# Residual adds by column halves, the last norm in pieces, and reciprocal roots as a power on GpSimd, in a two-layer hybrid decoder trunk

## The chip, the core and the metric

The kernel runs on one core of a Trainium2 chip. The metric is the device time of one execution in microseconds, as the median of several runs. The engines are TensorE (PE in the profile; its weight loads are PEld), VectorE (DVE), ScalarE (ACT), GpSimd (POOL) and SyncE (SP), which here only issues DMAs. A q behind an engine's name (SPq, ACTq) is its sequencer, which issues DMAs and waits on semaphores.

## The reference

256 tokens of 1024 columns go through two layers. Layer 0 mixes with sparse attention in two head groups, layer 1 with multi-head latent attention; after each comes a channel mixer (PEER) that fetches from 16384 experts. Every part reads a root-mean-square norm of the residual x and adds its result to x; one more norm gives the output:

```python
def rms_norm(x, g):
    xf = x.astype(jnp.float32)
    y = xf * lax.rsqrt(jnp.mean(xf * xf, axis=-1, keepdims=True) + NORM_EPS)
    return (y * g.astype(jnp.float32)).astype(x.dtype)

    for i in range(DEPTH):
        h = rms_norm(x, attn_norm[i])
        x = x + mixer(h)          # even_mixer, then mla_mixer
        h = rms_norm(x, ffn_norm[i])
        x = x + peer_ffn(h, peer_w_q[i], peer_sub_keys[i], peer_u[i], peer_v[i])
    return rms_norm(x, final_norm)
```

The latent attention norms two inner vectors as well, one of 768 and one of 256 columns. So the kernel takes seven sets of reciprocal roots: four of x ahead of the four parts, two inner ones, and the last norm's.

## The kernel before

The residual stays in the core's memory as four tiles x[tb][j]: two blocks tb of 128 tokens, each in two column halves j of 512. All weights stream once from HBM (320 MB). `Weights` loads units of up to 1024 columns into three raw buffers and splits them half by half, four halves ahead, into two float32r parts hi (ScalarE, L69) and lo (VectorE, L70), five buffers of each kind. A product is three matmuls: hi times hi, hi times lo, lo times hi.

The four stages run one behind the other: `even_mixer`, `peer`, `mla_mixer`, `peer`. Each of them ends in the same way. The mixers (`OutProj`) and the channel mixer (`peer`, `mm`, L1069 to L1074) accumulate their output in four PSUM tiles, one for each (tb, j). The last two chunks, that is four halves of weights (chunk 1 j 0, chunk 1 j 1, chunk 2 j 0, chunk 2 j 1), go through `last4` (L82): all four for tb 0, and then all four for tb 1. After each token block `add_to_x` (L460) adds two accumulators to x on VectorE, one instruction for each j (L463). During tb 1 one more half is split after each product.

The next stage starts with `to_T` (L284): TensorE transposes chunks of 128 columns of x for both token blocks (L288), ScalarE and VectorE write them as hi and lo. The PSUM pool of a stage is closed before that of the next one is opened.

`x_rstd` (L270) takes the squares of x on ScalarE with sums (L275) and calls `rsqrt` (L248): on VectorE it scales the sums, makes a first guess by an integer shift, and takes three Newton steps, column by column. The result is used late: by the rope tables (`scaled`, L343) in the mixers, by the scores' copy (L1024) and the normed tokens (`normed`, L794 and L795) in `peer`. `mla_mixer` calls `rsqrt` for its inner norms (L672, L675).

At the end `finish` (L808) loads the last gain, calls `x_rstd` for each token block, multiplies x by the gain on GpSimd (L817, four products), scales one half on ScalarE (L820) and the other on VectorE (L821), and issues four stores on SP (L823).

The kernel is written with the Tile framework. It sets the semaphores and orders the instructions of each engine's queue by a planner: by readiness in a simulated time line and by priority, which is the order of the code, save that the splits are moved up by 100 (`HP`) and the adds onto x by 200. So an engine's order in the trace isn't always that of the code.

## Time and profile before

| | |
|---|---|
| median of 3 runs | 1945.64 us (1944.63 to 1948.22) |
| profiled execution, span | 1945.3 us |
| PE busy | 1917.9 us (99%) |
| DVE busy | 1454.4 us (75%) |
| ACT busy | 1264.2 us (65%) |
| POOL busy | 6.4 us, 10 instructions |
| HBM read | 319.97 MB, 165 GB/s over the span |

The span goes from the first to the last instruction of one execution. A busy engine is one that has an instruction in flight, so PE's 99% counts the time in which it is fed, and also that in which its clock is granted at half rate. What can be taken out of the span is above all the time in which PE has nothing. The stages lie in the span at about 0 to 148 us (mixer of layer 0), to 980 (PEER), to 1101 (mixer of layer 1), to 1934 (PEER), and the rest is the last norm.

### The profile page before, as it was taken

What the parts mean: (1) busy time and instruction counts of PE and PEld (TensorE: products, weight loads), DVE (VectorE), ACT (ScalarE), POOL (GpSimd) and SP (SyncE); (2) the same over time, 40 slices, a digit from 0 to 9 for tenths busy, and PEclk for the clock granted to TensorE, in tenths of its full rate; (3) what the DMA queues carried; (4) which work ended last, traced back from release to release, by engine and by line L of the source; (5) the groups of instructions that cost most, each with busy time, mean ns of one, the idle gap of its engine ahead of it and who ended that gap; (6) DMA issues with size and microseconds to landing.
All of it is one profiled execution on the core that took longest, in us unless ns stands there. A gap on an engine that the chain in (4) does not pass through costs nothing.

```text
span 1945.3 us, 35740 instructions
## 1 busy us (share of the span) xinstructions
PE 1917.9 (99%) x12588; PEld 1727.7 (89%) x12588; DVE 1454.4 (75%) x3710; ACT 1264.2 (65%) x3060; POOL 6.4 (0%) x10
## 2 busy tenths in 40 slices
PE   8999999999999999999999999999999999999997
PEld 7769999999999888888888799999999998888886
DVE  7958998777788666666687699977778876666665
ACT  5556567887777555555576664688877765555554
POOL 0000000000000000000000000000000000000001
PEclk9989999999999999999999999999999999999999
DMA  6425565444444555555554345654444456666664
GB/s 186 128 65 164 172 195 166 154 151 152 152 152 153 194 192 190 192 192 190 189 168 131 120 150 177 195 163 152 144 152 152 154 171 191 190 194 193 188 193 141
DMA packets 90179, 323.33 MB, mean 166 GB/s; under 512 B 10512, under 2 KB 10896, under 8 KB 89744
## 3 DMA queue, kind: packets, MB, share of 16 engines
q1 hardware_dynamic: 88704, 318.71, 51.4%
q8 instruction: 99, 1.62, 0.3%
q0 software_dynamic: 288, 2.10, 0.3%
q14 instruction: 80, 0.66, 0.1%
q10 hardware_dynamic: 1008, 0.25, 0.1%
HBM read 319.97 MB, written 1.05 MB: 165 GB/s over the span
## 4 chain that ended last, share of the span: by engine, by line
PE 94%; DVE 3%; DMA 1%; ACT 1%; issue 1%; ACTq 0%; DVEq 0%
PE S L804 13%; PE S L805 13%; PE S L806 13%; PE acc L1072 12%; PE acc L1073 12%; PE acc L1074 12%; PE scp L984 6%; PE pj L301 2%; PE pj L303 2%; PE pj L302 2%; PE bk L372 1%; DVE lo L70 1%; DMA raw<-in_pu 1%; PE pj L438 1%; PE scp L1021 1%; PE pj L439 1%
## 5 line engine op out<-in xcount | busy, mean ns | idle before, releaser
L69 ACT ACTIVATE hi<-raw 128x512 fp32r<-128x512 f32 (+2 forms) x1214 | 763.2, 634 | 589.8 <-DVE lo L70 196.5
L70 DVE TENSOR_TENSOR lo<-raw,hi 128x512 fp32r<-128x512 f32 (+2 forms) x1214 | 827.1, 686 | 377.4 <-ACT hi L69 368.5
L804 PE MATMUL S<-hi,hi 128*128 128x256 f32 x2048 | 584.2, 285 | 1.9 <-ACT A L1013 1.8
L806 PE MATMUL S<-hi,lo 128*128 128x256 f32 x2048 | 573.4, 280 | 0.5 <-DVE lo L70 0.3
L805 PE MATMUL S<-lo,hi 128*128 128x256 f32 x2048 | 572.9, 280 | 0.0
L804 PEld LDWEIGHTS S<-hi,hi 128*128 128x128 f32 x2048 | 389.4, 190 | 3.1 <-ACT A L1013 2.9
L806 PEld LDWEIGHTS S<-hi,lo 128*128 128x128 f32 x2048 | 386.4, 189 | 1.3 <-DVE lo L70 1.2
L805 PEld LDWEIGHTS S<-lo,hi 128*128 128x128 f32 x2048 | 387.3, 189 | 0.0
L1073 PE MATMUL acc<-lo,ohA 128*128 128x512 f32 x512 | 200.2, 391 | 0.0
L1073 PE MATMUL acc<-lo,ohB 128*128 128x512 f32 x512 | 200.2, 391 | 0.0
L1074 PE MATMUL acc<-hi,ohA 128*128 128x512 f32 x512 | 199.4, 390 | 0.0
L1074 PE MATMUL acc<-hi,ohB 128*128 128x512 f32 x512 | 198.7, 390 | 0.0
L1072 PE MATMUL acc<-hi,ohB 128*128 128x512 f32 x512 | 160.5, 393 | 0.0
L1072 PE MATMUL acc<-hi,ohA 128*128 128x512 f32 x512 | 160.5, 393 | 0.0
L984 PE MATMUL scp<-ohA,ohB 128*128 128x128 f16 x1024 | 143.1, 296 | 0.0
L951 ACT ACTIVATE ohB<-ohB,RA 128x128 bf16<-128x128 bf16 x256 | 134.5, 654 | 0.0
L1074 PEld LDWEIGHTS acc<-hi,ohB 128*128 128x128 f32 x512 | 96.1, 188 | 22.0
L1074 PEld LDWEIGHTS acc<-hi,ohA 128*128 128x128 f32 x512 | 96.1, 188 | 22.0
L1072 PEld LDWEIGHTS acc<-hi,ohA 128*128 128x128 f32 x512 | 96.2, 188 | 20.8
L1072 PEld LDWEIGHTS acc<-hi,ohB 128*128 128x128 f32 x512 | 96.2, 188 | 20.7
L1073 PEld LDWEIGHTS acc<-lo,ohA 128*128 128x128 f32 x512 | 96.2, 188 | 20.3
L1073 PEld LDWEIGHTS acc<-lo,ohB 128*128 128x128 f32 x512 | 96.2, 188 | 20.2
(263 smaller groups left out, 2524.8 us busy)
## 6 DMA issues: line engine op xcount, KB each, us to landing
raw<-in_pu SPq DMA_DIRECT2D x256, 512.0 KB, 3.6
raw<-in_pv SPq DMA_DIRECT2D x256, 512.0 KB, 4.1
raw<-in_pq SPq DMA_DIRECT2D x32, 512.0 KB, 3.5
raw<-in_w SPq DMA_DIRECT2D x20, 512.0 KB, 3.7
raw<-in_uq SPq DMA_DIRECT2D x9, 512.0 KB, 4.3
raw<-in_w SPq DMA_DIRECT2D x12, 352.0 KB, 2.9
raw<-in_w0o SPq DMA_DIRECT2D x8, 512.0 KB, 3.6
raw<-in_w1o SPq DMA_DIRECT2D x8, 512.0 KB, 3.5
```

What stands on the lines that cost most here:

```text
L69: self.nc.scalar.activation(hi[:, :w], src, AF.Copy)
L70: self.nc.vector.tensor_tensor(lo[:, :w], src, hi[:, :w].bitcast(F32), op=OP.subtract)
L301: nc.tensor.matmul(ps[tb], hi[c][:, t], a, start=st, stop=False)
L302: nc.tensor.matmul(ps[tb], hi[c][:, t], b, start=False, stop=False)
L804: nc.tensor.matmul(p, a, hi[c], start=first and i == 0, stop=False)
L805: nc.tensor.matmul(p, a, lo[c], start=False, stop=False)
L806: nc.tensor.matmul(p, b, hi[c], start=False, stop=last and i == 3)
L951: nc.scalar.activation(e[:, :, j], e[:, :, j], AF.Relu, bias=r[1], scale=r[2])
L984: nc.tensor.matmul(p[:, i], E[:, 1, :, i], G[:, s, :, i], start=i + s == 0, stop=True, skip_group_check=True)
L1072: nc.tensor.matmul(o, a[:, 0, t], w[0], start=b == 0, stop=False)
L1073: nc.tensor.matmul(o, a[:, 0, t], w[1], start=False, stop=False)
L1074: nc.tensor.matmul(o, a[:, 1, t], w[0], start=False, stop=b == NK - 1)
```

## The change

Four things are changed; docstrings and comments are left out too, which changes nothing.

`last4` goes by column halves: for j 0 the two halves of weights of that j for tb 0 and then for tb 1, then the same for j 1. After each pair (tb, j) one accumulator is added to x. The next weights are still split during tb 1, now two in the first column half and two in the second.

`rsqrt` runs on GpSimd: it adds the parts, scales them and adds the epsilon, and raises the result to the power -0.5. VectorE's Newton steps are gone.

`finish` gives back a function that is called after each add onto x: the square and the sum of that piece, for j 0 the product with the gain on GpSimd, and for j 1 the root, the scaling of both halves and the stores. The second half is multiplied by root and gain in one instruction of VectorE.

The stores go out on two queues, the first column half's on ScalarE's, the second's on SP's.

```diff
     def last4(self, products):
-        j = self.pos
+        k = self.pos
         w = [self.next(self.look - i) for i in range(4)]
-        for tb in range(2):
-            for i in range(4):
-                products(i, w[i], tb)
-                if tb == 1:
-                    self.split(j + self.look + 1 + i)
-            yield tb
+        for j in range(2):
+            for tb in range(2):
+                for i in (j, j + 2):
+                    products(i, w[i], tb)
+                    if tb == 1:
+                        k += 1
+                        self.split(k + self.look)
+                yield tb, j
...
+        mhalf = cp.tile([128, 1], F32, name="mhalf")
+        nc.gpsimd.memset(mhalf, -0.5)
+
         def rsqrt(parts, n, name):
             k = parts[0].shape[1]
             v = small.tile([128, k], F32, name=name + "v")
-            nc.vector.tensor_scalar(v, parts[0], 1.0 / n, EPS, op0=OP.mult, op1=OP.add)
+            s = parts[0]
             for p in parts[1:]:
-                nc.vector.scalar_tensor_tensor(v, p, 1.0 / n, v, op0=OP.mult, op1=OP.add)
+                nc.gpsimd.tensor_tensor(v, s, p, op=OP.add)
+                s = v
+            nc.gpsimd.tensor_scalar(v, s, 1.0 / n, EPS, op0=OP.mult, op1=OP.add)
             y = small.tile([128, k], F32, name=name + "y")
-            t = small.tile([128, k], F32, name=name + "t")
-            nc.vector.tensor_single_scalar(t.bitcast(U32), v.bitcast(U32), 1, op=OP.logical_shift_right)
-            nc.vector.tensor_scalar(y.bitcast(I32), t.bitcast(I32), -1.0, float(0x5F3759DF), op0=OP.mult, op1=OP.add)
-            for c in (3.0, 12.0, 768.0):
-                for i in range(k):
-                    nc.vector.scalar_tensor_tensor(t[:, i:i + 1], y[:, i:i + 1], v[:, i:i + 1], y[:, i:i + 1],
-                                                   op0=OP.mult, op1=OP.mult)
-                for i in range(k):
-                    nc.vector.scalar_tensor_tensor(y[:, i:i + 1], t[:, i:i + 1], -c, y[:, i:i + 1],
-                                                   op0=OP.add, op1=OP.mult)
-            nc.vector.tensor_scalar(y, y, -1.0 / 8192, None, op0=OP.mult)
+            nc.gpsimd.tensor_tensor(y, v, mhalf[:, :1].to_broadcast([128, k]), op=OP.pow)
             return y
...
-                for tb in W.last4(lambda i, w, tb: self.mm(cs[i // 2], w, tb, i % 2, i >= 2)):
-                    add_to_x(tb, lambda j: self.ps[tb][j])
-
-        def add_to_x(tb, src):
-            for j in range(2):
-                with tc.high_priority(offset=2 * HP):
-                    nc.vector.tensor_tensor(x[tb][j], x[tb][j], src(j), op=OP.add)
+                for tb, j in W.last4(lambda i, w, tb: self.mm(cs[i // 2], w, tb, i % 2, i >= 2)):
+                    add_to_x(tb, j, self.ps[tb][j])
+
+        def add_to_x(tb, j, src):
+            with tc.high_priority(offset=2 * HP):
+                nc.vector.tensor_tensor(x[tb][j], x[tb][j], src, op=OP.add)
...
                 def finish():
-                    gf = rawp.tile([128, 1024], F32, name="raw")
-                    nc.sync.dma_start(gf, bass.AP(tensor=I["fin"].tensor, offset=I["fin"].offset, ap=[[0, 128], [1, D]]))
-                    r = [x_rstd(ps2.tile([128, 512], F32, name="S"), (tb,)) for tb in range(2)]
-                    ys = [rawp.tile([128, 1024], F32, name="raw") for tb in range(2)]
                     h = [slice(j * 512, (j + 1) * 512) for j in range(2)]
-                    for tb in range(2):
-                        for j in range(2):
-                            nc.gpsimd.tensor_tensor(ys[tb][:, h[j]], x[tb][j], gf[:, h[j]], op=OP.mult)
-                    for tb in range(2):
-                        y = ys[tb]
-                        nc.scalar.activation(y[:, h[0]], y[:, h[0]], AF.Copy, scale=r[tb])
-                        nc.vector.tensor_scalar(y[:, h[1]], y[:, h[1]], r[tb], None, op0=OP.mult)
-                        for j in range(2):
-                            nc.sync.dma_start(out[tb * 128:(tb + 1) * 128, h[j]], y[:, h[j]])
+                    ssq = small.tile([128, 2, 2], F32, name="fssq")
+                    t = {}
+
+                    def part(tb, j):
+                        if not t:
+                            t["g"] = rawp.tile([128, 1024], F32, name="raw")
+                            nc.sync.dma_start(t["g"], bass.AP(tensor=I["fin"].tensor, offset=I["fin"].offset, ap=[[0, 128], [1, D]]))
+                            t["y"] = [rawp.tile([128, 1024], F32, name="raw") for _ in range(2)]
+                        g, y = t["g"], t["y"][tb]
+                        nc.scalar.activation(ps2.tile([128, 512], F32, name="S"), x[tb][j], AF.Square,
+                                             accum_out=ssq[:, tb, j:j + 1])
+                        if j == 0:
+                            nc.gpsimd.tensor_tensor(y[:, h[0]], x[tb][0], g[:, h[0]], op=OP.mult)
+                            return
+                        r = rsqrt([ssq[:, tb, 0:1], ssq[:, tb, 1:2]], D, f"fin{tb}")
+                        nc.scalar.activation(y[:, h[0]], y[:, h[0]], AF.Copy, scale=r)
+                        nc.vector.scalar_tensor_tensor(y[:, h[1]], x[tb][1], r, g[:, h[1]], op0=OP.mult, op1=OP.mult)
+                        for i in range(2):
+                            (nc.sync, nc.scalar)[1 - i].dma_start(out[tb * 128:(tb + 1) * 128, h[i]], y[:, h[i]])
+
+                    return part
...
-                for tb in W.last4(lambda i, w, tb: mm(NK - 2 + i // 2, ws[i // 2], w, tb, i % 2)):
-                    add_to_x(tb, lambda j: acc[tb][j])
-                if final:
-                    finish()
+                last = finish() if final else None
+                for tb, j in W.last4(lambda i, w, tb: mm(NK - 2 + i // 2, ws[i // 2], w, tb, i % 2)):
+                    add_to_x(tb, j, acc[tb][j])
+                    if final:
+                        last(tb, j)
```

## Rows read from the trace of the kernel before

**Rows 1.** The head of the profile's page: span, busy time of each engine with its share and number of instructions.

```profile
span 1945.3 us, 35740 instructions
PE 1917.9 (99%) x12588; PEld 1727.7 (89%) x12588; DVE 1454.4 (75%) x3710; ACT 1264.2 (65%) x3060; POOL 6.4 (0%) x10
```

**Rows 2.** The waits of PE over the whole span: engine, line, what ended the wait, us in total, times, longest us. The list has ten rows; the other eight name a load (L189), the transposed tokens (L290, L291), PEER's activations (L1013, L1041), the attention's exponentials (L383) and the splits (L70).

```profile
PE scp L288 <- DVE x L463: 3.6, 2, 1.9
...
PE bk L288 <- DVE x L463: 1.5, 1, 1.5
```

**Rows 3.** The timeline of PE at the three seams between stages, the first transposes of the next stage: start us, us, engine, line, operation, out<-in, shape, count, and in brackets the idle time before it and what ended it.

```profile
149.76 0.66 PE L288 MATMUL scp<-ident,x 128*128 128x128 f32 x4 [1.72 <-DVE x L463]
...
981.38 0.87 PE L288 MATMUL bk<-ident,x 128*128 128x128 f32 x6 [1.46 <-DVE x L463]
...
1102.64 0.55 PE L288 MATMUL scp<-ident,x 128*128 128x128 f32 x3 [1.86 <-DVE x L463]
```

**Rows 4.** The timeline of DVE at the same seams; L463 adds onto x, L70 splits weights.

```profile
148.43 0.68 DVE L70 TENSOR_TENSOR lo<-raw,hi 128x512 fp32r<-128x512 f32 x1
149.03 0.68 DVE L463 TENSOR_TENSOR x<-x,pj 128x512 f32<-128x512 f32 x1
...
979.61 0.52 DVE L70 TENSOR_TENSOR lo<-raw,hi 128x352 fp32r<-128x352 f32 x1
980.04 1.28 DVE L463 TENSOR_TENSOR x<-x,acc 128x512 f32<-128x512 f32 x2
...
1100.10 1.28 DVE L70 TENSOR_TENSOR lo<-raw,hi 128x512 fp32r<-128x512 f32 x2
1101.31 1.28 DVE L463 TENSOR_TENSOR x<-x,pj 128x512 f32<-128x512 f32 x2
```

**Rows 5.** The timeline of all engines at the end of the program. In PE's rows ohB is block 126 and ohA block 127 of the activations.

```profile
1931.34 0.39 PE L1074 MATMUL acc<-hi,ohB 128*128 128x512 f32 x1
...
1932.45 2.06 DVE L463 TENSOR_TENSOR x<-x,acc 128x512 f32<-128x512 f32 x3 [3.68 <-PE acc L1074]
...
1933.17 0.60 ACT L275 ACTIVATE S<-x 128x512 f32<-128x512 f32 x1 [5.13 <-DVE x L463]
1933.28 4.98 POOL L817 TENSOR_TENSOR raw<-x,raw 128x512 f32<-128x512 f32 x4 [831.65 <-DVE x L463]
...
1933.86 0.39 PE L1074 MATMUL acc<-hi,ohA 128*128 128x512 f32 x1
...
1934.49 0.68 DVE L463 TENSOR_TENSOR x<-x,acc 128x512 f32<-128x512 f32 x1
...
1935.26 0.60 ACT L275 ACTIVATE S<-x 128x512 f32<-128x512 f32 x1
...
1935.80 0.18 ACT L275 ACTIVATION_READ_ACCUMULATOR S<-x 128x1 f32 x1
...
1940.27 0.15 DVE L267 TENSOR_SCALAR xn1y<-xn1y 128x1 f32<-128x1 f32 x1
```

**Rows 6.** Two lines of the reciprocal root on DVE, and the last norm's scaling on ACT, over the whole span: count, duration ns min/median/max, first and last start us. xn2 is the root of x ahead of the stages, xn1 that of the last norm.

```profile
L254 DVE SCALAR_TENSOR_TENSOR xn2v<-ssq,xn2v x4: 160/161/163, 16.5 to 1113.8; 128x2 f32<-128x2 f32 x4
L254 DVE SCALAR_TENSOR_TENSOR xn1v<-ssq,xn1v x2: 484/704/925, 1935.4 to 1936.1; 128x1 f32<-128x1 f32 x2
L262 DVE SCALAR_TENSOR_TENSOR xn2t<-xn2y,xn2v x24: 210/214/219, 17.6 to 1116.5; 128x1 f32<-128x1 f32 x24
L262 DVE SCALAR_TENSOR_TENSOR xn1t<-xn1y,xn1v x6: 211/217/1296, 1937.0 to 1939.5; 128x1 f32<-128x1 f32 x6
...
L820 ACT ACTIVATE raw<-raw,xn1y x2: 722/722/722, 1939.7 to 1940.5; 128x512 f32<-128x512 f32 x2
```

**Rows 7.** DMA issues: the last store on SP, the time from an issue of the stores to its landing, and an issue on ACT's queue from the program's start.

```profile
1941.55 0.46 SPq L823 DMA_DIRECT2D out_dram<-raw  x1
DMA to landing us min/median/max: 2.1/2.4/2.7
0.74 0.41 ACTq L189 DMA_DIRECT2D ident<-in_ident  x1
```

**Rows 8.** POOL: a fill of 128x1, the two loads of the keys, and the groups of line 817.

```profile
0.28 0.10 POOL L1144 MEMSET const-float32-1.0<- 128x1 f32 x1
148.35 0.72 POOL L781 DMA_DIRECT2D A<-in_sk  x1 [147.91 <-PE pj L440]
1101.10 0.53 POOL L781 DMA_DIRECT2D A<-in_sk  x1 [952.02 <-PE pj L440]
L817 POOL TENSOR_TENSOR raw<-x,raw x4: 1250/1264/1298, 1933.3 to 1937.0; 128x512 f32<-128x512 f32 x4
L817 POOLq MODIFY_POOL_CONFIG  x2: 37/37/37, 1101.6 to 1101.7; - x2
```

**Rows 9.** The timeline of DVE at the root of x in layer 0's mixer: the first step behind the sums, the last one, and the first readers.

```profile
16.49 0.16 DVE L254 SCALAR_TENSOR_TENSOR xn2v<-ssq,xn2v 128x2 f32<-128x2 f32 x1 [0.17 <-ACT bk L275]
21.02 0.16 DVE L267 TENSOR_SCALAR xn2y<-xn2y 128x2 f32<-128x2 f32 x1
21.21 0.42 DVE L343 TENSOR_SCALAR t<-C,xn2y 128x64 f32<-128x64 f32 x2
24.25 0.35 DVE L329 TENSOR_TENSOR rt<-pj,t 128x64 f32<-128x64 f32 x2
```

**Rows 10.** A stretch of layer 0's attention: start:end, us, then busy time (and instructions) of PE, PEld, DVE, ACT, POOL, then PE's granted clock, the DMA share and GB/s.

```profile
112.10:125.80 13.70, 13.70 (x36) 6.81 (x36) 6.24 (x16) 6.31 (x26) 0.00 (x0) 0.50 0.00 0
```

## The prediction

> **What bounds the kernel now.** I read the page first: TensorE is busy 1917.9 of 1945.3 us, VectorE 75%, ScalarE 65%, GpSimd 0% [rows 1]. So only time in which TensorE stands still is to be had, 27.4 us in all. Next the list of TensorE's waits, to see who ends them: on the x adds (L463) it waits 3.6 and 1.5 us, and no line of the reciprocal root (L252 to L267) stands in it [rows 2]. Third, TensorE's rows around those waits: at the three seams between layers' halves it ends a block, stands 1.72, 1.46 and 1.86 us, and starts the next transposes [rows 3]: 5.04 us together. Last the end of the program: TensorE's last matmul ends at 1933.86 + 0.39 = 1934.25, the span at 1945.3. These 11.05 us are the largest stretch without TensorE, and nothing hides any of it [rows 5].
>
> **The tail before, step by step.** The last x add starts 0.24 us after the last matmul and takes 0.68; from the start of an x add to the start of the square on it are 0.72 (1932.45 to 1933.17); a square with its accumulator read takes 0.72 (1935.26 to 1935.98). Then come VectorE's Newton chains of both token blocks, in one queue, until 1940.42 [rows 5]. Their first steps are not at their own price: L254 took 0.48 and 0.93 us and L262 1.30 us, beside medians of 0.16 and 0.21 in the other stages [rows 6]; in just that time GpSimd ran its four 1.25 us products (1933.28 to 1938.26). Then one scaling (ScalarE 0.72 [rows 6]), four DMA issues one behind the other on SP, and 2.1 to 2.7 us from an issue to its landing; the last one, issued at 1941.55, landed at about 1944.25, and 1.05 us later the span ends [rows 5, 7].
>
> **The tail after.** The order of the last four blocks matters. The trace shows that TensorE doesn't run them as written: all of block 126 comes first, then the pieces of block 127, so the four accumulators end about 0.69 us apart and the adds start 0.69 us apart [rows 5]. I keep that spacing for the new order (tb0 j0, tb1 j0, tb0 j1, tb1 j1). Call the end of the last matmul T and one root on GpSimd R (add, scale and bias, power; all 128x1, one behind the other). Sum of squares of tb0: its second accumulator ends at T - 0.69, + 0.24 + 0.72 + 0.75 = T + 1.02. Of tb1: T + 0.24 + 0.72 + 0.75 = T + 1.71. Both roots go through one GpSimd queue, so the second is ready at T + 1.02 + 2R once R is above 0.7. Behind it: 0.05 hand-over, 0.72 scaling on ScalarE, 0.02 to the issue, 2.4 to the landing (the median), 1.05 to the end: T + 5.26 + 2R. GpSimd's products with the gain are now two instead of four and lie ahead of T (two times 1.25 us, from about T - 1.1 on, the second over at about T + 1.4; the first root may lose 0.4 to it at worst), and no VectorE step of a chain runs beside them. The second half's product with gain and root is one VectorE instruction of two SBUF operands: nearest row L70, 0.69 us, beside the 0.72 on ScalarE, so it costs nothing; if ScalarE's half were gone it would be the bound, at the same price. The stores now go from two queues, half of them from ScalarE's: an issue there takes 0.41 [rows 7]. For tb0 it sits behind the scaling in ScalarE's queue, ends at about T + 1.02 + R + 0.05 + 0.72 + 0.41, and the last scaling isn't ready before T + 1.07 + 2R: hidden from R = 1.13 on, a few tenths below that.
>
> **The price R.** The trace has no power and no small GpSimd arithmetic. Its bounds: three operations at the price of a 128x1 fill (0.10 us) give 0.3; three at the price of a 128x512 product (1.25 to 1.30) give 3.8 [rows 8]. I take 1.2: add and scale at 0.2 each, nearest to the fill because the shape is the same; the power 0.7, between the ends because it is a function and not one pass; 0.1 for hand-overs. Then the tail is 5.26 + 2.4 = 7.66 us, a gain of 3.4. At 0.3 the chain is set by tb1 alone (T + 1.71 + R + 4.24 = T + 6.25): gain 4.8. At 3.8 it is T + 12.9: a loss of 1.8.
>
> The Trainium skill, "GPSIMD Engine Reference", section on elementwise cycle accounting, gives 4497 ns for a two-input add of 2048 elements; with this trace's 1.26 us at 512 an estimate from the two is 0.18 us for an instruction with hardly any elements, and by it R would be 0.55 and the time 1939.7. The page has no price for a power, and no run here shows one yet.
>
> **The seams.** All of the 24 matmuls stay; only their order changes. The 5.04 us hold two things: the wait for the last x add, and VectorE work queued in front of it. With nothing in front, the wait is 0.24 + 0.68 + 0.05 = 0.97. In the trace it is longer because a weight split (L70, 0.60 us a step) sits between the adds: at 149.03 and 980.04 the last adds follow one, at 1101.31 they follow two [rows 4]. Now the adds go one at a time as column halves end, and only one is left at T. The splits still come as buffers come free, two of the next stage's in the first half. With no split in front of the last add: 3 x 0.97 = 2.9, a gain of 2.1. With one in front each time: 3 x 1.57 = 4.7, a gain of 0.3. With two: 6.5, a loss of 1.5. I take the middle of the first two, a **gain of 1.2**. I don't credit that the first transposes need only column halves j = 0: in all three seams they read chunks 0 to 3, that is x of j = 0 alone, and still start 0.05 us after the last add of all [rows 3, 4]. So they wait for the old PSUM pool as a whole, and will again.
>
> **The roots in the middle.** Each x norm loses 17 small VectorE instructions (about 3 us), the two inner norms 16 and 18. Valued at nothing: TensorE never waits for them [rows 2], and the root is used late. What is new is a wait: VectorE's scaled tables (L343), and VectorE's and ScalarE's normed tokens (L795, L794), now wait for GpSimd with weight splits queued behind them. In layer 0 the root took 16.49 to 21.18 on VectorE, 4.7 us [rows 9], so a GpSimd root under 4.7 us is earlier than before. Behind a longer one VectorE holds up the splits, with up to four halves split ahead as cover. GpSimd is empty but for the key loads issued at 148.35 and 1101.10, 0.72 and 0.53 us each [rows 8]. The added fill of -0.5 goes among the fills of the first microsecond. The earlier release of two weight buffers costs nothing.
>
> **Sum.** 3.4 + 1.2 = 4.6 us. The span of 1945.3 becomes 1940.7; the median of the runs before is 1945.64, 0.3 above that span, so 1941.0.
>
> **Rivals.**
> *The root is dear, or queued badly*: R = 2.2 gives a tail of 9.66, gain 1.4, in all 2.6: 1943.0. ScalarE putting tb0's scaling in front of tb1's last square gives the same order of size: square from T + 3.0, end at T + 9.2, total gain 3.1: 1942.5. For it: the power is unseen, and the code gives the scaling first. Against: by its readiness the square (T + 0.96) comes before.
> *Slower, by the root's wait*: at R = 7 the tail is 19.3, 8.2 longer, less 1.2: 1952.6; if the four x norms also hold their queues by 7 - 4.7 each, 9.2 more: 1961.8. It is slower by over 0.2% from R = 5.5 on (5.26 + 2R = 11.05 + 1.2 + 3.9). For it: two MODIFY_POOL_CONFIG stand in GpSimd's queue for L817, 832 us before that line runs, so what such a load costs is hidden here [rows 8]. Against: the four products then took 1.25 to 1.30, the first no longer than the others.
> The Trainium skill, same page, section on instruction dispatch, says that the first call of a freshly loaded GpSimd kernel pays about 6 us. If that falls on the first root only, the tables at 21.21 would be some 2.5 us late, in front of readers from 24.25 on [rows 9], and the time stays near the forecast; on every root it is this rival.
> *The seams open fully*: if the transposes do start on column half 0, the 5.04 us go whole: 1937.2. Against it is the 0.05 us in all three seams.
> *TensorE's clock*: in layer 0's attention it is granted 0.50 for 13.7 us, from 112.1 to 125.8 [rows 10]; that costs up to 6.85. Another order of the queues could drop it (1934.2) or add one (1947.8). Nothing in the change touches that stage directly.
>
> **Chances.** Forecast 0.53, dear root or queue 0.24, slow root 0.06, open seams 0.08, clock 0.04 and 0.05. A measurement of this kernel tells about 0.2% (3.9 us) from no change, so faster means under 1941.7: about seven tenths of the forecast's 0.53, the open seams, and the clock's gain make some 0.5; I say 0.54, as the seams may give up to 0.9 more. Slower (over 1949.5): 0.06. Same: 0.40. The range from 1937.6 to 1945.2 takes in the root's price from 0.3 to 3 and the seams from 2.1 to nothing; it leaves out the slow root, the clock, and most of the open seams.
>
> **What would show it.** Right: the span ends about 7.7 us after the last matmul; a root on GpSimd of 1.2 us; VectorE without steps of 0.5 to 1.3 us on 128x1 tiles; TensorE's waits on the x adds near 3.8 in sum. Wrong: power steps above 1 us, a last square behind a scaling, x adds behind two splits, or a low clock at another place.

## The result, and the profile after

| | before | after |
|---|---|---|
| median of 4 runs, us | 1946.91 | 1967.49 |
| lowest to highest, us | 1944.63 to 1948.22 | 1965.65 to 1968.45 |
| profiled run: span and time, us | 1945.3 | 1963.9, 1965.65 |

The changed kernel takes 1.011 times as long (95% interval 1.0096 to 1.0125). The forecast was 1941.0 with a range up to 1945.2: it missed by 26.5 us, and slower had been given 6 in 100.

The head of the page after, beside [rows 1]:

```profile
span 1963.9 us, 35641 instructions
...
PE 1941.6 (99%) x12588; PEld 1736.7 (88%) x12588; DVE 1439.4 (73%) x3586; ACT 1266.2 (64%) x3060; POOL 14.5 (1%) x33
```

TensorE has as many instructions as before and is busy 23.7 us longer. VectorE has 124 fewer. So the time went into TensorE's own work and not into a wait. The list of TensorE's waits after says the same; its rows on the x adds were 3.6 and 1.5 us before [rows 2]:

```profile
PE scp L285 <- DVE x L459: 3.0, 2, 1.6
PE bk L285 <- DVE x L459: 1.6, 1, 1.6
```

Where did the time grow? This table is worked out from TensorE's timeline in both traces: for each stage, from the start of its first to the end of its last matmul. U are the stages of PEER's first product (weights stationary, 256 columns of tokens moving), V those of its second (the activations stationary, split into the buffers ohA/ohB, and 512 columns of weights moving).

| us | before | after | difference |
|---|---|---|---|
| before the first matmul | 4.58 | 4.08 | -0.50 |
| mixer 0 | 143.46 | 145.87 | +2.41 |
| U of layer 0 | 478.56 | 481.46 | +2.90 |
| V of layer 0 | 351.75 | 358.56 | +6.81 |
| mixer 1 | 119.40 | 120.36 | +0.96 |
| U of layer 1 | 480.01 | 481.74 | +1.73 |
| V of layer 1 | 351.75 | 358.56 | +6.81 |
| three seams | 5.04 | 4.53 | -0.51 |
| from the last matmul to the end | 11.01 | 9.02 | -1.99 |

The parts that the change was about did shrink. What grew is spread over all stages, most of it in the two V stages, by exactly the same amount in both. One stretch of 335 us, all of it inside the V stage of layer 0, shows it. Columns: start:end, us, busy us of PE (matmuls), granted clock, DMA share, GB/s. Before:

```profile
640.00:975.00 335.00, 335.00 (x1466) 1.00 0.59 191
```

After:

```profile
640.00:975.00 335.00, 335.00 (x1438) 1.00 0.58 188
```

TensorE is busy without a gap in both, at a granted clock of 1.00 (2.4 GHz) in both, and gets 28 matmuls less done. The groups of the same stretch by line, with mean ns of one; before:

```profile
L1073 PE MATMUL acc<-lo,ohB 128*128 128x512 f32 x245 | 95.8, 391 | 0.0
L1074 PE MATMUL acc<-hi,ohB 128*128 128x512 f32 x245 | 95.6, 390 | 0.0
...
L1072 PE MATMUL acc<-hi,ohB 128*128 128x512 f32 x244 | 76.0, 393 | 0.0
```

After:

```profile
L1078 PE MATMUL acc<-hi,ohB 128*128 128x512 f32 x239 | 95.1, 398 | 0.0
...
L1077 PE MATMUL acc<-lo,ohB 128*128 128x512 f32 x239 | 93.9, 393 | 0.0
L1076 PE MATMUL acc<-hi,ohA 128*128 128x512 f32 x240 | 75.4, 396 | 0.0
```

Idle time before them is 0.0, and each takes 2 to 8 ns more. From start to start a matmul of V takes 351.75 / 1536 = 229.0 ns before and 233.4 after. The code of these lines is the same. A stall at an edge of a stage can't do this: the rate of the engine itself is lower.

Of mixer 0's 2.41 us some 1.7 are put down to another thing, by an estimate: after has 3.4 us at a clock of 0.50 (1.2 GHz) that before lacks, and at half the clock half of them is lost. Ahead of it TensorE had no gap for 16 us, as in before, where no fall follows (start:end, us, then busy time of PE, PEld, DVE, ACT, POOL, clock, DMA share, GB/s):

```profile
76.70:80.10 3.40, 3.40 (x9) 2.27 (x9) 2.48 (x9) 1.86 (x8) 0.00 (x0) 0.50 0.17 69
```

It comes and goes: e1 below, whose instructions stand in the order of before, has it too, at 75.32, and g2, with the new order, has not. So it isn't put down to the change. Over all kernels here mixer 0 has 13.7 to 23.9 us at this clock, the stretch of [rows 10] counted, and takes 142.8 to 148.4 us; the 0.7 that are left lie within that spread.

**What moved without being named in the change.** The profile doesn't show where tiles lie in SBUF, but the compiled programs do, in bytes within a partition. The change adds the tile of -0.5 to the pool of constants, in front of the weights' buffers (32 bytes as allotted). In the pool of small tiles, behind the weights, it drops the t tiles of the Newton steps and gives the last norm other tiles, in sum 128 bytes less. What lies behind both is the stage region: tokens, activations A, ohA/ohB. So the tile of -0.5 moves weights and region alike, and only the small tiles change the distance between them.

| | weights' buffers (hi) | stage region (A) | distance |
|---|---|---|---|
| before | 40544 | 62496 | 21952 |
| after | 40576 | 62400 | 21824 |

### The profile page after: what moved, and what is told of

Read it like the earlier page. It is cut to its first block, busy times and chain, and to the rows that moved or that the text cites. A ratio compares the mean times of both kernels' runs of the same rounds, so it can differ in the third digit from the quotient of the medians.

```text
span 1963.9 us, 35641 instructions
## 1 busy us (share of the span) xinstructions
PE 1941.6 (99%) x12588; PEld 1736.7 (88%) x12588; DVE 1439.4 (73%) x3586; ACT 1266.2 (64%) x3060; POOL 14.5 (1%) x33
## 4 chain that ended last, share of the span: by engine, by line
PE 93%; DVE 5%; ACT 1%; issue 1%; DMA 0%; DVEq 0%; POOL 0%; POOLq 0%; ACTq 0%
PE S L802 12%; PE S L800 12%; PE S L801 12%; PE acc L1078 12%; PE acc L1076 12%; PE acc L1077 12%; PE scp L988 6%; PE pj L298 2%; PE pj L300 2%; PE pj L299 2%; DVE lo L70 2%; PE bk L369 1%; DVE A L836 1%; DVE A L833 1%; PE pj L435 1%
## 5 line engine op out<-in xcount | busy, mean ns | idle before, releaser
L70 DVE TENSOR_TENSOR lo<-raw,hi 128x512 fp32r<-128x512 f32 (+2 forms) x1214 | 825.0, 684 | 407.3 <-ACT hi L69 395.4
L1078 PE MATMUL acc<-hi,ohA 128*128 128x512 f32 x512 | 203.4, 398 | 0.0
L1078 PE MATMUL acc<-hi,ohB 128*128 128x512 f32 x512 | 202.8, 398 | 0.0
L1076 PE MATMUL acc<-hi,ohB 128*128 128x512 f32 x512 | 161.6, 395 | 0.0
L1076 PE MATMUL acc<-hi,ohA 128*128 128x512 f32 x512 | 161.3, 395 | 0.0
L988 PE MATMUL scp<-ohA,ohB 128*128 128x128 f16 x1024 | 143.2, 296 | 0.0
```

The costliest lines, as they stand in the source:

```text
L70: self.nc.vector.tensor_tensor(lo[:, :w], src, hi[:, :w].bitcast(F32), op=OP.subtract)
L988: nc.tensor.matmul(p[:, i], E[:, 1, :, i], G[:, s, :, i], start=i + s == 0, stop=True, skip_group_check=True)
L1076: nc.tensor.matmul(o, a[:, 0, t], w[0], start=b == 0, stop=False)
L1078: nc.tensor.matmul(o, a[:, 1, t], w[0], start=False, stop=b == NK - 1)
```

## The experiments

The theory from here on is placement. Rivals: the new order of the last blocks and adds slows something (rival 1), or GpSimd's roots do (rival 2).

### e1 to e4: move the buffers, change nothing else

e1 (at the place of the new tile), e3 and e4 in the kernel before, e2 in the kernel after:

```diff
+        pad = cp.tile([128, 1], F32, name="pad"); nc.gpsimd.memset(pad, -0.5)
```
```diff
-        mhalf = cp.tile([128, 1], F32, name="mhalf")
-        nc.gpsimd.memset(mhalf, -0.5)
+        mhalf = cp.tile([128, 16], F32, name="mhalf")
+        nc.gpsimd.memset(mhalf[:, :1], -0.5)
```
```diff
+        pad = cp.tile([128, 1], F32, name="pad"); nc.gpsimd.memset(pad, -0.5)
+        pads = small.tile([128, 1], F32, name="pads", bufs=1); nc.gpsimd.memset(pads, -0.5)
```
```diff
+        pads = small.tile([128, 1], F32, name="pads", bufs=1); nc.gpsimd.memset(pads, -0.5)
```

> The kernel before, with one more 128x1 tile in the constants' pool and its fill on GpSimd; nothing else. It moves every buffer behind it by 32 bytes within a partition: the weight buffers (raw, hi, lo) from 40544 to 40576, the stage region from 62496 to 62528, so that all of them start on a multiple of 64 bytes, as in the kernel after, where before all of them lie 32 bytes off one. Theory (placement): the extra time comes from where the matmuls' operands lie in SBUF, so the two V stages (351.75 us each before) take about 358.6, the 512-column matmuls come every 233 ns instead of 228.5, and the time goes up by about 18 us, to some 1965. Rival 1 (the new order of the last blocks and adds) and rival 2 (GpSimd's roots take something from TensorE): neither is in this kernel, so the V stages stay at 351.8 and the time within 2 us of before.

> The kernel after, with its tile of -0.5 made 16 columns wide instead of 1 (only the first is filled and read). All work and its order are those of the kernel after; the buffers lie 32 bytes further: weights at 40608, stage region at 62432, both 32 bytes off a multiple of 64, as in the kernel before. Theory (placement): the V stages return to 351.75 us and the rest too; with the tail 2.0 us and the seams 0.5 us shorter than before, as the profile after has them, and the start 0.5 earlier, the span is about 1942.5 and the median some 1943 (1941 to 1946 if the additional stretch at a clock of 0.5 in layer 0's mixer stays). Rivals 1 and 2: nothing they speak of is touched, so the V stages stay at 358.6 and the time at 1967.

> The kernel before with two unused tiles, one 128x1 in the constants' pool and one 128x1 in the pool of small tiles, each with its fill: weights at 40576 (on a multiple of 64 bytes, as after), stage region (tokens, one-hots, A) at 62560 (32 off one, as before). In the V stages the moving operand is the weights, in the U stages it is the tokens and the weights are loaded. If the moving operand's place decides: V about 358.6, U as before (478.6 and 480.0). If the stage region's place decides: V 351.75, U 481.5. If only weights against region counts (their distance): neither the times of before nor of after need come back. Rivals without placement: all stages as before.

> The kernel before with one unused 128x1 tile in the pool of small tiles: weights stay at 40544 (32 off a multiple of 64 bytes, as before), the stage region goes to 62528 (on a multiple of 64, as after). If the moving operand's place decides: V 351.75 us each, U about 481.5 (the tokens move). If the stage region's place decides for both: V 358.6. Rivals without placement: all stages as before, 1945 in all.

| | weights | region | distance to before | V, us | U, us | time, us |
|---|---|---|---|---|---|---|
| e1 | 40576 | 62528 | 0 | 351.75 | 477.5, 478.0 | 1945.36, ratio 0.9999 (0.9989 to 1.0009) |
| e2 | 40608 | 62432 | -128 | 358.56 | 481.2, 481.6 | 1967.25, ratio 1.0098 (1.0081 to 1.0115) |
| e3 | 40576 | 62560 | +32 | 358.56 | 483.2, 483.6 | 1973.42, one run |
| e4 | 40544 | 62528 | +32 | 358.56 | 483.1, 483.6 | 1971.87, one run |

The theory as first put, that a start on a multiple of 64 bytes is slow, fell in e1 and e2: both moved everything by 32 bytes, and neither time changed. But e3 and e4 are kernels before with an unused tile or two, and on TensorE, VectorE and ScalarE their instructions stand in the order of e1 and of before, all 12588, 3710 and 3060. Their V stages are as long as those of the kernel after, and U is longer still. The same stretch as above, in e1 and then in e4:

```profile
640.00:975.00 335.00, 335.00 (x1465) 1.00 0.60 191
```

```profile
640.00:975.00 335.00, 335.00 (x1437) 1.00 0.59 189
```

e1 and e4 even have their region at the same address, and e4 and before their weights. Neither place alone decides; the distance does. Rivals 1 and 2 can't act in e4, which holds nothing of the change but a shift.

### f1: the kernel after at the distance of before

```diff
         nc.gpsimd.memset(mhalf, -0.5)
+        pads = small.tile([128, 32], F32, name="pads", bufs=1); nc.gpsimd.memset(pads[:, :1], 0.0)
```

> The kernel after, all its work and order kept, with one unused tile of 128 bytes in the pool of small tiles (only one column of it is filled): the stage region goes from 62400 to 62528, the weights stay at 40576, so the distance from weights to region is again 21952, as in the kernel before and in e1 (after: 21824; e3 and e4: 21984). The two runs before this one left the first form of the theory (a multiple of 64) dead: e1 and e2 moved both by 32 bytes and changed nothing, e3 and e4 moved them against each other by 32 and had V stages of 358.56 us at an order of instructions equal to that of before. Theory now (distance): V 351.75 us each, U 477.5 to 480, 512-column matmuls in the mixers back by 5 ns, span about 1942 to 1943, median some 1943. Rivals (order of the last blocks, roots on GpSimd): V stays at 358.56, time 1967.

Measured: 1942.77 us, ratio to before 0.9984 (0.9975 to 0.9993); V 351.75 twice, U 477.3 twice. With one unused tile of 128 bytes the change is 24.7 us faster than as it was made, and 2.8 us faster than before.

```profile
640.00:975.00 335.00, 335.00 (x1465) 1.00 0.60 191
```

### s1 to s3: the distance in steps

The kernel before with a pad in front of the tokens and ohA/ohB of each PEER stage; 16 and 24 columns of 4 bytes in s1, 40 and 48 in s2, 56 and 64 in s3:

```diff
+                hpad = hp.tile([128, (16, 24)[layer]], F32, name="hpad")
                 hi, lo = tiles8(hp, "hi"), tiles8(hp, "lo")
...
                 nc.gpsimd.dma_start(sk, I["sk"][layer])
+                nc.gpsimd.memset(hpad[:, :1], 0.0)
```

> The kernel before with a pad ahead of the tokens and one-hot tiles of each PEER stage: 64 bytes in layer 0, 96 in layer 1 (one more fill on GpSimd in each). So the distance from weights to tokens and ohA/ohB is 64 bytes more in layer 0 and 96 in layer 1, and mixers and A are untouched. Known so far for V: +0 gives 351.75, +32 and -128 give 358.56. Theory (distance of stationary to moving operand): V changes at these places alone, to one of the levels seen or a new one, the mixers stay at 143.5 and 119.4. If it is A (the activations) against the weights instead: V stays 351.75. A period of 64 or 128 bytes is already out, since -128 is slow.

> As s1, with 160 bytes in layer 0 and 192 in layer 1. Theory: V at one of the levels of distance; if the operands meet in a window around +0 with a period of 256, then 192 and 160 are slow like 32 and -128. If A against the weights decides: V 351.75 in both.

> As s1, with 224 bytes in layer 0 and 256 in layer 1. Theory with a period of 256: layer 1's V is 351.75 and its U 480, layer 0's V tells whether the fast place is one step of 32 bytes wide or more. With a longer period: 256 gives 358.56. If A against the weights decides: V 351.75 in both.

Measured, with the stages seen so far:

| bytes more than before | V, us | ns a matmul | U, us |
|---|---|---|---|
| 0 (before, e1, f1) | 351.75 | 229.0 | 477.3 to 480.0 |
| 32 (e3, e4) | 358.56 | 233.4 | 483.1 to 483.6 |
| 64 (s1) | 348.35 | 226.8 | 487.9 |
| 96 (s1) | 358.56 | 233.4 | 482.9 |
| -128 (after, e2) | 358.56 | 233.4 | 481.2 to 481.7 |
| 160 (s2) | 360.01 | 234.4 | 488.3 |
| 192 (s2) | 357.09 | 232.5 | 486.9 |
| 224 (s3) | 358.57 | 233.4 | 482.7 |
| 256 (s3) | 351.75 | 229.0 | 478.4 |

The mixers stayed (143.2 to 144.3 and 119.4), as they had to, with nothing of theirs moved. At 256 the times of 0 are back; a period of 64 or 128 is out, as 64 and -128 differ from 0. One value was better than before: 64, for V alone. Of these steps the kernel before stood in the best place for U and the second best for V.

### g1 and g2: the change's parts alone, at the distance of before

g1 is the kernel before with the new rsqrt (and a pad of 64 columns among the small tiles); g2 the kernel after with the old rsqrt (and a pad of 16):

```diff
-            nc.vector.tensor_scalar(v, parts[0], 1.0 / n, EPS, op0=OP.mult, op1=OP.add)
...
+            nc.gpsimd.tensor_scalar(v, s, 1.0 / n, EPS, op0=OP.mult, op1=OP.add)
...
+            nc.gpsimd.tensor_tensor(y, v, mhalf[:, :1].to_broadcast([128, k]), op=OP.pow)
```
```diff
-            nc.gpsimd.tensor_tensor(y, v, mhalf[:, :1].to_broadcast([128, k]), op=OP.pow)
...
+            nc.vector.tensor_scalar(y, y, -1.0 / 8192, None, op0=OP.mult)
```

> The kernel before with the change's roots alone (add, scale and bias, power on GpSimd in place of VectorE's Newton steps); the last blocks, the adds and the last norm are those of before. A tile of 256 bytes among the small ones puts the stage region at 62528 with the weights at 40576, so the distance is 21952 as before. Theory (the loss was distance alone, the roots in the middle are worth nothing): V 351.75, seams 5.0 in sum as before. The tail: the four products with the gain end about 4.0 us after TensorE's last matmul as before; the roots behind them on GpSimd take 2.2 more, then 0.72 for the scaling and 3.5 to the end, so 10.4 us beside 11.0 before; if the roots go first and the products behind them, 13. Time between 1944 and 1948. Rival (the roots slow something in the stages): V or U longer than 351.75 and 480.

> The kernel after with the roots of before (Newton steps on VectorE); the last blocks by column halves, the single adds and the last norm in pieces stay. A tile of 64 bytes among the small ones makes the distance 22208, which is 21952 + 256; 256 more gave V 351.75 in the run with 256 bytes ahead of the tokens. Theory (distance): V 351.75, U 478 to 480, seams 0.3 to 0.5 shorter than before. Tail: both chains of Newton steps on VectorE take about 4.4 us behind the last sum of squares (1.7 after the last matmul), then 0.72 and some 3.5 to 4.5: 10.3 to 11.3, so GpSimd's roots carry most of the tail's 2.0. Time 1944 to 1947. Rival (order of the last blocks slows V): 358.56 and 1965.

| us | before | g1, roots | g2, halves and pieces | f1, both |
|---|---|---|---|---|
| time, median | 1945.6 | 1945.70 | 1942.62 | 1942.77 |
| ratio (interval) | | 1.0002 (0.9993 to 1.0011) | 0.9986 (0.9977 to 0.9995) | 0.9984 (0.9975 to 0.9993) |
| V | 351.75 | 351.75 | 351.75 | 351.75 |
| three seams | 5.04 | 5.04 | 4.72 | 4.72 |
| tail | 11.01 | 11.06 | 9.46 | 9.03 |

Rivals 1 and 2 are dead: neither part lengthens U or V. The roots alone bring nothing, where 0.6 us of the tail had been expected of them. In g1's tail (timeline, GpSimd and the first reader) they stand behind all four products:

```profile
1932.64 4.96 POOL L813 TENSOR_TENSOR raw<-x,raw 128x512 f32<-128x512 f32 x4 [815.74 <-DVE x L459]
...
1937.56 0.34 POOL L257 TENSOR_TENSOR xn1v<-ssq 128x1 f32<-128x1 f32 x2
...
1938.52 1.10 POOL L261 TENSOR_TENSOR xn1y<-xn1v,mhalf 128x1 f32<-128x1 f32 x2
1939.10 1.33 ACT L816 ACTIVATE raw<-raw,xn1y 128x512 f32<-128x512 f32 x2 [3.79 <-POOL xn1y L261]
```

The tail's gain comes from the pieces, 1.55 us of it with Newton's steps kept (two products on GpSimd instead of four, and the chains start earlier), and 0.43 more with the roots; g2's expectation had it the other way, with most of the gain from the roots. The medians of g2 and f1 can't tell that 0.43.

### g3: 64 bytes for ohA/ohB, and one product off GpSimd

On f1: a pad ahead of act, ohA and ohB (raw tokens and A1 lie behind them and move along), and the tail regrouped.

```diff
+                ohpad = ohp.tile([128, 16], F32, name="ohpad", bufs=1)
...
-                        if j == 0:
+                        if j == 0 and tb == 0:
                             nc.gpsimd.tensor_tensor(y[:, h[0]], x[tb][0], g[:, h[0]], op=OP.mult)
+                        if tb == 0 or j == 0:
                             return
+                        nc.vector.tensor_tensor(y[:, h[0]], x[1][0], g[:, h[0]], op=OP.mult)
+                        for b in range(2):
...
```

> f1 with two things more. First a pad of 64 bytes ahead of the act and ohA/ohB tiles alone: the V stages' stationary operand lies 64 bytes further (V 348.35 in s1), the tokens of the U stages stay where U was shortest. Second, in the last norm the product with the gain for the first half of token block 1 goes to VectorE, behind its last add, and each root is issued whole before the next: GpSimd has one product and then the two roots one after the other. Theory: V 348.35 each (only ohA/ohB moved, so it is their distance to the weights), U about 477.5 as in f1. Tail: first root from 1.1 to 2.2 us behind the last matmul, second to 3.3, scaling 0.72, then 2.6 + 1.05: 7.7 us beside 9.0 in f1. Time 6.8 + 1.3 below f1's 1942.8: 1934.7. If the tokens' place or A's decided V: V 351.75, time 1941.5.

Measured: 1939.37 us, ratio 0.9969 (0.9959 to 0.9980). V 348.32 twice, as expected: the tokens in front of the pad need not move for V, and j1 below shows that its own parts in ohA/ohB are enough. U was 480.2 and 480.0, 2.9 and 2.6 above f1, which was not expected. The tail was 8.57, not 7.7. Its timeline shows what went wrong:

```profile
1929.34 0.69 DVE L825 TENSOR_TENSOR raw<-x,raw 128x512 f32<-128x512 f32 x1
...
1929.96 0.68 DVE L460 TENSOR_TENSOR x<-x,acc 128x512 f32<-128x512 f32 x1
...
1931.53 0.73 POOL L261 TENSOR_TENSOR fin1v<-fssq 128x1 f32<-128x1 f32 x1
```

The last matmul ended at 1929.15, so the last add could start at 1929.4; the product, meant to stand behind it, was put in front, and the add waited 0.6 us. The second root's first step then took 0.73 us, where after's took 0.19. The stores, now in two pairs 1.76 us apart, landed in 2.6 to 2.8 us, where after's four together took 2.7 to 3.4:

```profile
DMA to landing us min/median/max: 2.6/2.7/2.8
```

### h1, i2, i3: which operands

h1 is the kernel before with only the lo halves of the weights moved by 32 bytes (the region by 256). i3 is the kernel before with only a1 moved by 32; a1 is the rest part of each split block of activations, the counterpart of lo, and a0 the other. i2 is h1 and i3 together. The V stages' order on TensorE within a half is hi, hi, lo, hi, lo, hi by what streams; by the rows of the weight loads (PEld) the next matmul's stationary tile is loaded from 3 ns after the start of a stream for 188 ns, and a1 (L1074) is the one loaded beside a lo (L1073). In the kernel before:

```profile
1926.30 0.39 PE L1073 MATMUL acc<-lo,ohA 128*128 128x512 f32 x1
1926.31 0.19 PEld L1074 LDWEIGHTS acc<-hi,ohA 128*128 128x128 f32 x1
```

```diff
+        lpad = lop.tile([128, 8], F32, name="lpad", bufs=1); nc.gpsimd.memset(lpad[:, :1], 0.0)
...
+        pads = small.tile([128, 56], F32, name="pads", bufs=1); nc.gpsimd.memset(pads[:, :1], 0.0)
```
```diff
+                    full = ohp.tile([128, 576], F32, name="ohA" if b % 2 else "ohB").bitcast(F32R)
+                    t = full[:, :256], full[:, 256 + 8:512 + 8]
```

> The kernel before with a pad of 32 bytes ahead of the lo halves of the weights and one of 224 among the small tiles, so that hi to region is 21952 + 256 (as before, by the period) and lo to region 32 less than that. In the V stages every third matmul streams lo, the others hi; while a matmul streams, the stationary tile of the next is loaded. Theory (the load of the stationary tile meets the stream of the moving one): only matmuls that stream lo change, to about 233.5 ns from 229 if -32 is like +32 or like 224 (358.57); those that stream hi stay near 229; V about 351.75 + 6.8 / 3 = 354.0. Rival (another thing than the stream of this operand, as VectorE's writes of lo or of the one-hot tiles against it): all three kinds change alike, or none.

> h1 with the second half of each ohA/ohB tile (the rest part, a1) moved by 32 bytes as well. In the V stages' order (hi, hi, lo, hi, lo, hi) the a1 of the next matmul is loaded just while lo streams, so each stream and the load beside it are at the distance of before, though lo and hi, and a1 and a0, are each 32 bytes apart from where they were. Theory (load against stream decides, and nothing else): V back to 351.75, or at least well below h1's 356.87. If hi against lo (two streams one behind the other) decides: V 356.87 or more. If the load lies partly beside the next stream: between, as a1's load then also meets hi at 32.

> The kernel before with a1 alone moved by 32 bytes, the weights and all else in place (the tiles are 256 bytes longer each, which the period makes nothing). The mirror of h1: of the six matmuls of a half, the two that stream lo have a load at the distance of +32. Theory: V near h1's 356.87 (h1 had -32 on the same pairs), the added ns on the matmuls that stream lo and those behind them, none on the other hi. If the streams' own places decide: V 351.75. U 478 to 480 as before in any case.

Mean ns from a matmul's start to the next one's, by line, and the V stage:

| | first two (hi) | lo | hi behind lo | V, us | U, us |
|---|---|---|---|---|---|
| before | 230.4 | 228.8 | 227.5 | 351.75 | 478.6, 480.0 |
| h1: lo moved | 230.7 | 234.1 | 231.9 | 356.87 | 483.4, 483.7 |
| i3: a1 moved | 230.4 | 232.9 | 231.3 | 355.75 | 477.1, 479.9 |
| i2: both moved | 232.5 | 232.2 | 232.0 | 356.89 | 483.3, 483.6 |

h1 and i3 speak for the load meeting the stream: in each, the stream beside a1's load and the one behind it grew, and the first two not. (h1's expectation had left the one behind it as it was, with a V of 354.0; measured are 356.87.) i3 moved no streamed tile, so the loaded one counts by itself. But i2, in which every load is at its old distance from the stream beside it, should then have come back, and was as long as h1. So the plain rule of one load and one stream fell; the times of i2 and h1 agree to 0.02 us, though the six matmuls share them otherwise, as if lo against hi (or a load against more than the stream beside it) counted as well. Which pairs count, and why, stays open. That the engines beside TensorE are in it has little room: of the intervals in which neither VectorE nor ScalarE ran an instruction, 22 in each kernel, those of e1 have a mean of 229.4 ns and those of e4 233.5, the same step as all the others (worked out from the three timelines).

### i1, j1, j2: the U stages of g3, and finer steps

i1 is g3 with raw tokens and A1 moved on to 256 bytes. j1 is g3 without its pad; instead the buffers ohA/ohB are 256 bytes longer, and V's parts start 64 bytes into them, while the gates' one-hots stay at the start. j2 is the kernel before with V's parts 16 bytes in (layer 0) and 48 (layer 1).

```diff
+                rpad = rawpool.tile([128, 48], F32, name="rpad")
...
+                apad = pa.tile([128, 48], F32, name="apad")
```
```diff
-                    t = ohp.tile([128, 4, 128], F32, name="ohA" if b % 2 else "ohB").rearrange("p (s h) e -> p s (h e)", s=2).bitcast(F32R)
+                    t = ohp.tile([128, 576], F32, name="ohA" if b % 2 else "ohB")[:, 16:512 + 16].rearrange("p (s t) -> p s t", s=2).bitcast(F32R)
```
```diff
+                    t = ohp.tile([128, 576], F32, name="ohA" if b % 2 else "ohB")[:, (4, 12)[layer]:512 + (4, 12)[layer]].rearrange("p (s t) -> p s t", s=2).bitcast(F32R)
```

> g3 with a pad of 192 bytes behind the ohA/ohB tiles, so that the raw tokens and the activation blocks A1, which g3 had moved by 64 bytes along with the one-hot tiles, are moved by 256 in all, which is none by the period. In g3 the U stages took 480.1 beside 477.3 in f1, though the tokens that most of U reads had not moved. Theory (raw tokens or A1 at the wrong distance made U longer): U 477.3 again, V 348.3, time 5 us below g3's 1939.4: 1934. Rival (U's length differs from kernel to kernel by some 2.5 us for another reason, as between the two U stages of the kernel before, 478.6 and 480.0): U 478 to 480 and 1937 to 1940.

> g3 without its pad ahead of the act and one-hot tiles. Instead the ohA/ohB tiles are 256 bytes longer, and the V stages' stationary parts stand 64 bytes into them, while the one-hots of the gates, which use the same buffers in the U stages, start where they did in f1, as act, tokens and A1 do (by the period). Theory (in g3 and i1 the moved act and one-hot tiles made U 2.5 longer): V 348.3 each and U 477.3 as in f1, so 5 us less than g3: 1934 to 1935. Rival (U's length follows the order or something else that g3 has over f1): U 479.8 and 1939.

> The kernel before with ohA/ohB tiles 256 bytes longer, the V stages' stationary parts 16 bytes into them in layer 0 and 48 in layer 1; all else in place, U as before (477 to 480). Known at +0, +32, +64: 351.75, 358.56, 348.35. If V's length follows the distance in steps of 32 bytes: 351.75 in layer 0 and 358.56 in layer 1. If it follows finer: between or outside of these.

| | V, us | U, us | time, us |
|---|---|---|---|
| i1 | 348.32, 348.32 | 479.8, 479.9 | 1940.49, ratio 0.9978 (0.9968 to 0.9987) |
| j1 | 348.32, 348.32 | 477.9, 478.6 | 1934.92, ratio 0.9942 (0.9929 to 0.9956) |
| j2 | 356.28, 348.35 | 477.4, 478.9 | 1948.50, one run |

i1's theory fell: with raw tokens and A1 back in place U stayed as long as in g3. j1 came out as expected, 10.5 us below before and 32.6 below the kernel after, the fastest of the study. In it U is 1.4 to 2.3 below g3's; but U ranges from 477.1 to 480.0 among the kernels at the old distance too, so that part isn't settled by one profile each. j2 shows that the distance counts finer than in 32 bytes (16 gives 356.28, between 351.75 and 358.56), and that 48 is as good as 64. The stretch of V in j1:

```profile
640.00:975.00 335.00, 335.00 (x1480) 1.00 0.58 192
```

## Why the prediction was wrong

**The step that failed** is "All of the 24 matmuls stay; only their order changes", and with it "only time in which TensorE stands still is to be had". Work that stays was taken to keep its price. The sum had no term for TensorE's own rate, and no rival had one (the clock rival came nearest, and in U, V and mixer 1 the clock was 1.00). What moved the distance, the 128 bytes less of small tiles, stands nowhere in the prediction. The fill that it valued at nothing, "The added fill of -0.5 goes among the fills of the first microsecond", is worth nothing: its tile moves weights and region alike, as in e1.

Measured between the profiles of f1 and after, the term is 13.6 us in V, 8.6 in U and 0.9 in mixer 1; against before it is 13.6, 4.6 and 1.0. U is the less certain, as its stages at the old distance differ by up to 2.9 us among themselves. For mixer 0 it stays open: after takes 145.87 us, kernels at the old distance with as much time at a clock of 0.50 (17.1 us) take 143.9 to 145.6, and f1, with 20.5 us of it, 147.33. Between the profiled spans of after and f1 the difference is 1963.9 - 1942.5 = 21.4 us, between their medians 1967.49 - 1942.77 = 24.7. e4 shows it without the change, f1 the change without it.

The Trainium skill, "SBUF — State Buffer", section "Who interferes with whom", gives TensorE two read ports of its own, one for the moving operand and one for the weight load, and says that it never waits on anyone. By that rule the distance would cost nothing. The runs here disagree: 226.8 to 234.4 ns a matmul, at one order of instructions and a clock of 1.00. The measurement decides; that one of the two ports holds up the other is not shown, since i2 went against the simplest form of it.

**The seams: right in kind, too large.** A gain of 1.2 us was forecast, the middle of two cases; it is 0.51 after and 0.32 in f1, which is the case of one split in front of the last adds (0.3). VectorE and TensorE at the three seams after, beside [rows 3, 4]:

```profile
149.66 0.68 DVE L70 TENSOR_TENSOR lo<-raw,hi 128x512 fp32r<-128x512 f32 x1
...
150.26 1.27 DVE L459 TENSOR_TENSOR x<-x,pj 128x512 f32<-128x512 f32 x2
...
151.59 0.66 PE L285 MATMUL scp<-ident,x 128*128 128x128 f32 x4 [1.64 <-DVE x L459]
...
991.27 0.52 DVE L70 TENSOR_TENSOR lo<-raw,hi 128x352 fp32r<-128x352 f32 x1
991.71 1.28 DVE L459 TENSOR_TENSOR x<-x,acc 128x512 f32<-128x512 f32 x2
...
993.04 1.10 PE L285 MATMUL bk<-ident,x 128*128 128x128 f32 x8 [1.58 <-DVE x L459]
...
1112.17 1.29 DVE L70 TENSOR_TENSOR lo<-raw,hi 128x512 fp32r<-128x512 f32 x2
...
1113.38 1.28 DVE L459 TENSOR_TENSOR x<-x,pj 128x512 f32<-128x512 f32 x2
...
1114.71 0.65 PE L285 MATMUL scp<-ident,x 128*128 128x128 f32 x4 [1.31 <-DVE x L459]
```

The last two adds still come as a pair behind a split, at the third seam behind two, where the step "only one is left at T" had one add. That the transposes wait for the last add of all, and not for column half 0, held in all three.

**The tail: the sums on time, the end not.** T, the end of the last matmul, is 1954.46 + 0.40 = 1954.86. Timeline after, beside [rows 5]:

```profile
1953.03 2.69 DVE L459 TENSOR_TENSOR x<-x,acc 128x512 f32<-128x512 f32 x4 [3.78 <-PE acc L1078]
...
1953.85 2.53 POOL L819 TENSOR_TENSOR raw<-x,raw 128x512 f32<-128x512 f32 x2 [825.43 <-DVE x L459]
...
1956.35 0.19 POOL L260 TENSOR_TENSOR fin0v<-fssq 128x1 f32<-128x1 f32 x1
1956.36 0.19 ACT L816 ACTIVATION_READ_ACCUMULATOR S<-x 128x1 f32 x1
1956.63 0.19 POOL L260 TENSOR_TENSOR fin1v<-fssq 128x1 f32<-128x1 f32 x1
...
1957.45 0.55 POOL L264 TENSOR_TENSOR fin0y<-fin0v,mhalf 128x1 f32<-128x1 f32 x1
1957.97 0.55 POOL L264 TENSOR_TENSOR fin1y<-fin1v,mhalf 128x1 f32<-128x1 f32 x1
...
1958.66 0.71 ACT L822 ACTIVATE raw<-raw,fin1y 128x512 f32<-128x512 f32 x1
...
1958.78 0.98 ACTq L825 DMA_DIRECT2D out_dram<-raw  x2
1958.81 1.01 SPq L825 DMA_DIRECT2D out_dram<-raw  x2
```

tb1's sum is ready at T + 1.69 (forecast 1.71). R is about right: 0.28 + 0.28 + 0.55 = 1.1 for a root by itself, forecast 1.2. But the first root waits for GpSimd's products until T + 1.49, and the two roots are interleaved, so they are ready at T + 3.14 and T + 3.66 (forecast 2.22 and 3.42), and the last scaling ends at T + 4.51 (forecast 4.19). Then the four stores are issued within 0.7 us on two queues, and landing takes longer than the 2.4 us of [rows 7]:

```profile
DMA to landing us min/median/max: 2.7/3.1/3.4
```

From the last issue at T + 4.62 to the end it is 4.40 us, forecast 3.45. That is the larger part of the miss: 9.02 instead of 7.66, a gain of 2.0 instead of 3.4. The landing had been priced by stores that one queue issued one behind the other.

**The roots in the middle: right.** In layer 0 the root is ready at 17.90, before at 21.18 [rows 9], and g1 shows that nothing is won by it:

```profile
16.17 0.19 POOL L260 TENSOR_TENSOR xn2v<-ssq 128x2 f32<-128x2 f32 x1 [15.35 <-ACT bk L272]
16.45 0.19 POOL L262 TENSOR_SCALAR xn2v<-xn2v 128x2 f32<-128x2 f32 x1
16.73 1.17 POOL L264 TENSOR_TENSOR xn2y<-xn2v,mhalf 128x2 f32<-128x2 f32 x1
```

The slow root didn't come: the first power took 1.17 us, and the later ones of that shape 0.69 to 1.19. The 6 us that the Trainium skill ("GPSIMD Engine Reference", "Instruction dispatch") gives for the first call of a freshly loaded kernel show at no root here. The trace can't rule them out, though: after's two MODIFY_POOL_CONFIG stand at 0.76 and 0.79 us, and GpSimd is idle from there to the first root at 16.17. The price of an add in the Trainium skill (same page, "Elementwise — side-by-side cycle accounting"), from which 0.18 us was estimated for a small instruction, fits: the add and the scale took 0.19.

With placement held, the time would have come out in the range of 1937.6 to 1945.2, but not for all of its reasons. f1 takes 1942.77; of the 4.6 us that the parts were to bring it has 2.3 (tail 2.0, seams 0.3), and in its profile U is 3.9 us shorter than before's and mixer 0 as much longer. The changed kernel's 1967.49 lies far outside.

Two sums of the prediction are slightly off, without weight here. By its own rule for short roots, T + 1.71 + R + 4.24, an R of 0.55 gives 1939.9 and not 1939.7. And a root of 3 us with no gain at the seams gives about 1945.9, so the range up to 1945.2 doesn't hold both at once.

## What to carry to other kernels

When a kernel's TensorE is busy throughout, look first at what one matmul takes in a long stage, before and after, and at how many fit into the same stretch: a change of some per cent there outweighs every seam. An edit that adds or drops a tile of a few bytes moves all buffers behind it (e4: one unused tile, 1971.87 us); compare the addresses of the two programs, and hold the distance between stationary and moving operands with a pad before judging the edit itself. Then try a few distances on purpose: in this kernel a shift of 64 bytes of one operand is worth 6.9 us, more than the change that was meant to help.

## What had not been expected of the hardware

- The rate of 512-column matmuls follows the distance of their operands in SBUF, and the times are back at 256 bytes: 348.32 to 360.01 us for the same 1536 matmuls, and 16 bytes are enough to change it. The 256-column matmuls of U range from 477.1 to 488.3 us for a stage.
- The best distance for one stage is the worst but one for another (64 bytes: V 348.35, U 487.9, where 160 has 488.3), so each operand is best placed by itself, as j1 does.
- Four stores of 256 KB issued together on two queues landed in 2.7 to 3.4 us; in pairs 1.76 us apart in 2.6 to 2.8.
